# A four-layer transformer forward pass on one core: when a head's values run, when x rows are loaded, and how the decay and compressed-value products are shaped

## The chip, the core and the metric

The kernel runs on one core of a Trainium2 chip. A core has TensorE (matrix products, PE), VectorE (DVE), ScalarE (ACT), GpSimd (POOL) and SyncE (SP), each with a queue of its own that it works off in order, and DMA queues. The metric is device time in microseconds (us), lower is better. Before the change it is 2943.2 us, the median of three runs (2942.22 to 2947.26).

## The reference

One sequence of 512 tokens of 1024 values goes through two blocks of two layers each. The change touches the parts in bold.

```python
# first block: layer 0 mixes by dilated attention, layer 1 by a gated linear recurrence (LRU)
x = x + rms_norm(mixer(rms_norm(x, pre)), post)
x = x + rms_norm(conv_ffn(rms_norm(x, pre)), post)

# dilated attention: 3 groups of 8 heads of 128, each group with its own stride and band
logits = q k / sqrt(128) + bias, masked;  p = exp(logits - max);  o = p v / sum;  lse = max + log(sum)
alpha = softmax over the 3 groups of lse;  o = sum(alpha * o)          # then @ w_o

# conv_ffn: u = causal 3-tap convolution of x @ w_up; (gelu(g) * v) @ w_down

# second block, each layer: three mixers side by side
#   nsa:  8 heads, keys and values once compressed (blocks of 32), once selected, once in a window, gated
#   fox:  softmax(q k + c_i - c_j) v, c the running sum of log_sigmoid(f) of each head
#   memory: attention to 256 memory rows
```

In words: **the three groups of a head are merged by their maxima and sums**; **each layer ends with a norm, an addition to x and the next layer's norm**; **nsa adds the compressed values to the same accumulator as the other two**; **fox adds a decay c_i − c_j to each score**.

## The kernel before, in words

All large products run in three passes (`mm3`, L46 to L48): each operand is split into a high and a low part of the reduced fp32 format, and high by high, low by high and high by low are added in PSUM. A weight piece of 128 x 1024 is loaded by SP (`wunit`, L207), its high part cast by ScalarE (L197), its low part subtracted by VectorE (L198), or by POOL where the caller asks for it. `fms` (L218) makes products transposed, a column group at a time; the first call's group of several columns shares a pass over the tokens, and there the low parts of all columns but the first are made on POOL. `tm` (L238) makes the products that end a layer: four token blocks of 128, one PSUM bank each. `TOK_BANKS` (L38) names these: for the first half of the columns `acc`, `acc`, `acc`, `pv`. PSUM has three banks `acc`, two `sc`, two `tr` and one `pv`.

The program is written in the order of priority; a planner then lays out each engine's queue by its own simulated times. On the chip the engines keep that order and wait for each other by semaphores.

The attention (`dilated_attention`, L447) takes the query and key products of a head from `fms`, six of them (three groups, query and key), each 24 matmuls of 512 columns, 48 products in all. Scores of groups 1 and 2 (`DilatedHead.scores`, L79) are due one product after their group's key, those of group 0 one product after the head's last. A score adds the bias and takes the maximum on VectorE (L91, L100) and the exponential on ScalarE (L102). Groups order their rows differently, so the maxima and sums of each order (`own`) go to DRAM and come back in the other (L103, L104: `dx<-W` and `W<-dx`). `normalize` (L108) then works on the small tile `c`: VectorE L115 and L117, ScalarE L118 (exponential), VectorE to L122, and POOL scales `PA` and `PB`, the two orders' probabilities, by it (L126). `values` (L128) transposes these on TensorE (L136, L147), copies them out on ScalarE and VectorE, and multiplies them by the values into the bank `pv` (for the second order L155, L156), which VectorE adds to `oT` (L159). It is due `VALUES_AFTER` = 4 products after the head's last product. At the end all that is left is issued (`due(True)`, L494). `attn_layer` (L517) then splits `oT` and calls the output projection.

Each layer of the first block ends in `post_and_next` (L366): the product's first 512 columns for the four token blocks, then the second 512; from that, block by block, the sum of squares, the old x row (`x_load`, L352, two tiles in rotation, by SP), the new x (two operations at L390), its store, the next norm (L297 to L304), transposes (L312) and the split into the next layer's operands `hH`, `hL`.

In the second block the branches' work is woven with the products that build it. `fox` adds the decay to each score by a third matmul (L1268) of 4 rows: two rows hold the negated running sum's parts against ones, two the running sum's own. The four heads of a half lie at partitions 0, 32, 64 and 96, and the matmul names its place by `tile_position`. `decay` (L1277) fills the tile `A` of ones (POOL) and puts the rows in by eight DMAs per layer. `nsa` adds the compressed values by matmuls of 32 rows at `tile_position` (L1117), two per half of a head.

`colvec` (L267) loads up to 128 rows of a vector and transposes them (L277) to columns; `bias_tables` (L401) builds the relative bias with a table `oh` (L415).

Of the kernel before, what the change touches and what calls it, by code (L numbers as in the profile page):

```python
# [10 lines left out]
F32 = mybir.dt.float32  # L11
# [19 lines left out]
AHEAD = 0  # L31
VALUES_AFTER = 4
# [5 lines left out]
TOK_BANKS = (("acc", "acc", "acc", "pv"), ("sc", "sc", "tr", "tr"))  # L38
# [123 lines left out]
class Net:  # L162
    def __init__(self, ctx, tc, ins, out):
# [16 lines left out]
        self.junk = self.cp.tile([128, 512], mybir.dt.bfloat16, name="junk")  # L180
# [36 lines left out]
    def fms(self, w, cols, rh, rl, n=128, kt=KD, group=1, eng=None):  # L217
# [5 lines left out]
        q, ahead = 0, []  # L223
# [14 lines left out]
    def tm(self, w, col, n, lh, ll, kt=KD, banks=0, tail=0):  # L238
# [28 lines left out]
    def colvec(self, rows, name):  # L267

        nc = self.nc
# [6 lines left out]
        ps = self.bank("tr")  # L276
        nc.tensor.transpose(ps[:, :R], st, self.ident[:R, :R])  # L277
        out = self.vp.tile([128, R], F32, name=name)
        nc.vector.tensor_copy(out, ps[:, :R])
        return out  # L280
# [69 lines left out]
    def x_load(self, t):  # L350
        xt = self.ep.tile([128, D], F32, tag="nx", bufs=2, name="x")
        self.nc.sync.dma_start(xt, self.x[t * 128:(t + 1) * 128])  # L352
        return xt
# [12 lines left out]
    def post_and_next(self, w, lh, ll, kt, vectors, nxt, spare):  # L366
# [80 lines left out]
    def dilated_attention(self, qkv):  # L447
# [3 lines left out]
        oT = self.op.tile([128, KD, T], F32, tag="oT", bufs=1, name="oT")  # L451
# [18 lines left out]
        for hd in range(8):  # L470
# [22 lines left out]
            after(VALUES_AFTER, values, a)  # L493
        due(True)  # L494
        return oT

    def first_rows(self, g):

        with self.tc.tile_pool(name="edge", bufs=1) as self.ep:
            xs = [self.x_load(t) for t in range(2)]  # L500
# [3 lines left out]
            for t in range(NT):  # L504
                xt = xs[t] if t < 2 else self.x_load(t)
# [11 lines left out]
    def attn_layer(self, g_next, nxt):  # L517
        i, tc = self.i, self.tc
        with tc.tile_pool(name="attO", bufs=1) as self.op:
            self.ep = self.op  # L520
            with tc.tile_pool(name="attA", bufs=2) as self.ap:
                vs = self.post_vectors(i["norm_mix_post"][0], g_next)
                oT = self.dilated_attention(self.attn_qkv(self.h))
# [3 lines left out]
            with tc.tile_pool(name="attE", bufs=1) as self.ep:  # L527
                return self.post_and_next(i["attn_w_o"][0], *self.rows(oh), KD, vs, nxt,
                                          lambda i: self.ep.tile([128, T], F32, name=f"spare{i}"))
# [12 lines left out]
    def vectors(self):  # L542
# [4 lines left out]
        for l in range(2):  # L547
# [3 lines left out]
            for k, r in enumerate(rows):  # L551
                cols.append(self.colvec([r], f"cw{k}_{l}"))
# [3 lines left out]
        cv = self.colvec([i["lru_conv_w"][0].rearrange("k (r p) -> (k r) p", p=128), v8(i["lru_conv_b"][0]),  # L556
                          i["lru_ga_b"][0].rearrange("n (r p) -> (n r) p", p=128),
                          i["lru_gx_b"][0].rearrange("n (r p) -> (n r) p", p=128), v8(i["lru_lambda"][0])], "lrucv")
# [23 lines left out]
    def ffn_layer(self, l, up, g_next, nxt):  # L582
        nc, i, tc = self.nc, self.i, self.tc
        nf = FF // 128
        with tc.tile_pool(name=f"ffn{l}", bufs=1) as fp:
# [4 lines left out]
            for m in range(nf):  # L590
                u = []
                for c in (m, nf + m):
                    ps = next(up)
                    t = fp.tile([128, T], F32, tag="cv", bufs=6, name="cv")
                    self.conv(t, ps, lambda k: cw[k][:, c:c + 1], cb[:, c:c + 1], 3)
                    u.append(t)
                g, v = u
                nc.scalar.activation(g, g, AF.Gelu_apprx_tanh)
                nc.gpsimd.tensor_tensor(g, g, v, op=OP.mult)  # L599
                self.split(aH[m], aL[m], g)  # L600
            return self.post_and_next(i["ffn_w_down"][l], lambda k, t: aH[k][:, t * 128:(t + 1) * 128],
# [40 lines left out]
    def lru_layer(self, lin, g_next, nxt):  # L642
        nc, i, tc = self.nc, self.i, self.tc
        with tc.tile_pool(name="lru", bufs=1) as lp:
# [79 lines left out]
            ll = lambda k, t: xs[k // 2][1][:, k % 2, t * 128:(t + 1) * 128]  # L724
            return self.post_and_next(i["lru_w_out"][0], lh, ll, KD, self.post_vectors(i["norm_mix_post"][1], g_next), nxt, lambda i: lt("spare"))
# [84 lines left out]
    def zblocks(self, w, blocks, lh, ll, toks=NT):  # L810
# [8 lines left out]
        for t in range(toks):  # L819
            for (col, n, use), un in zip(blocks, us):  # L820
# [5 lines left out]
                zc = self.lt("zc", [128, n])  # L826
                nc.scalar.copy(zc, ps[:, :n])
                use(t, zc)
# [191 lines left out]
    def nsa(self, l, h, w_in, os):  # L1020
# [15 lines left out]
        def cmp_kv(t, z):  # L1036
# [16 lines left out]
        def key_value(br):  # L1053
            def use(t, z):
# [4 lines left out]
                if br == 1:  # L1059
                    nc.scalar.activation(gate[:, t], z[:, 256:280], AF.Tanh, scale=0.5)  # L1060
# [7 lines left out]
        def query(g):  # L1068
            def use(t, z):
# [23 lines left out]
        for p in range(4):  # L1093
            of = self.lt("of", [128, T])
            sl = self.silu2(l, h, OFF_NSILU + p * 128)
            for e in range(2):
                hd = 2 * p + e
                g, r = hd // 4, hd % 4
                for half in range(2):
# [15 lines left out]
                    rs = slice(32 * r, 32 * r + 32)  # L1115
                    for uu in range(2):
                        nc.tensor.matmul(ps[:, :256], VC[rs, g], PTC[rs, uu, g, hs], start=False, stop=False, tile_position=(32 * r, 0))  # L1117
# [5 lines left out]
    def compress(self, l, XT, gk):  # L1123
# [4 lines left out]
        VC = self.lt("VC", [128, 2, 128], F32R)  # L1128
        G = []
        for a, nm in ((0, "k"), (1, "v")):  # L1130
            pes = self.lt("pes", [16, 128])
# [322 lines left out]
```

## Time and profile before

| | before |
|---|---|
| median of three runs (lowest, highest) | 2943.2 us (2942.22, 2947.26) |
| the profiled execution: its time, its span | 2946.58 us, 2944.8 us |
| TensorE busy | 2816.7 us, 96% of the span |
| VectorE, ScalarE, POOL busy | 1647.3, 1303.5, 667.2 us |
| mean granted clock of TensorE | 0.979 |
| chain that ended last: PE, DVE, DMA, issue | 81%, 6%, 6%, 3% |

The profile is of one execution. "Busy" counts an engine's instructions, not its waiting. The chain that ended last is followed back from the last instruction, at each step to what released it. A wait is written as the waiting instruction, an arrow, and what ended the wait; "issue" is time in which nothing that the profile shows held the engine back. `PEclk` is the clock that TensorE was granted, 1.00 being full. Lines such as L136 are lines of the kernel. TensorE's matmuls overlap: the distance between starts tells what one costs, while its duration is longer.

### The profile page before, as it was taken

What the parts mean: (1) busy time and instruction counts of PE and PEld (TensorE: products, weight loads), DVE (VectorE), ACT (ScalarE), POOL (GpSimd) and SP (SyncE); (2) the same over time, 40 slices, a digit from 0 to 9 for tenths busy, and PEclk for the clock granted to TensorE, in tenths of its full rate; (3) what the DMA queues carried; (4) which work ended last, traced back from release to release, by engine and by line L of the source; (5) the groups of instructions that cost most, each with busy time, mean ns of one, the idle gap of its engine ahead of it and who ended that gap; (6) DMA issues with size and microseconds to landing.
All of it is one profiled execution on the core that took longest, in us unless ns stands there. A gap on an engine that the chain in (4) does not pass through costs nothing.

```text
span 2944.8 us, 40532 instructions
## 1 busy us (share of the span) xinstructions
PE 2816.7 (96%) x15005; PEld 2393.2 (81%) x15005; DVE 1647.3 (56%) x3232; ACT 1303.5 (44%) x2564; POOL 667.2 (23%) x754
## 2 busy tenths in 40 slices
PE   8998988799999997999999999999999999999999
PEld 7877777678888786888888898788888898788887
DVE  4235454465552459655524776666645667666653
ACT  4223343344442364444423654665533554665542
POOL 1001010121110225211101242334321352333320
PEclk9999999899999998999999999999999999999999
DMA  5453333153332342533323424112234423112233
GB/s 178 150 167 83 80 97 68 58 158 94 100 95 99 112 123 66 164 94 100 94 100 125 138 67 113 34 51 73 68 91 134 146 67 106 40 51 73 62 93 108
DMA packets 392317, 288.47 MB, mean 98 GB/s; under 512 B 33640, under 2 KB 351992, under 8 KB 392120
## 3 DMA queue, kind: packets, MB, share of 16 engines
q1 hardware_dynamic: 383120, 269.04, 31.7%
q10 hardware_dynamic: 9000, 16.85, 1.6%
q8 instruction: 119, 1.95, 0.3%
q14 instruction: 78, 0.64, 0.1%
HBM read 266.73 MB, written 21.07 MB: 98 GB/s over the span
## 4 chain that ended last, share of the span: by engine, by line
PE 81%; DVE 6%; DMA 6%; issue 3%; ACT 2%; POOL 2%; ACTq 0%; SPq 0%; DVEq 0%; POOLq 0%
PE acc L46 19%; PE acc L48 19%; PE acc L47 19%; PE tr L804 3%; DMA dx<-W 2%; PE pv L864 2%; PE sc L46 2%; PE sc L47 2%; PE sc L48 2%; PE tr L46 1%; PE tr L48 1%; PE tr L47 1%; PE pv L48 1%; PE pv L47 1%; PE pv L46 1%
## 5 line engine op out<-in xcount | busy, mean ns | idle before, releaser
L198 DVE TENSOR_TENSOR wl<-ws,wh 128x1024 fp32r<-128x1024 f32 (+4 forms) x456 | 543.3, 1192 | 620.0 <-ACT wh L197 615.8
L197 ACT CAST wh<-ws 128x1024 fp32r<-128x1024 f32 (+2 forms) x476 | 469.3, 986 | 724.9 <-PE acc L47 283.4
L46 PE MATMUL acc<-hH,wh 128*128 128x512 f32 (+1 forms) x1928 | 752.1, 391 | 23.1 <-ACT hH L197 13.6
L48 PE MATMUL acc<-hH,wl 128*128 128x512 f32 (+1 forms) x1928 | 748.1, 388 | 2.5 <-POOL wl L198 2.5
L47 PE MATMUL acc<-hL,wh 128*128 128x512 f32 (+1 forms) x1928 | 748.2, 388 | 1.0 <-DVE hL L198 0.9
L46 PEld LDWEIGHTS acc<-hH,wh 128*128 128x128 f32 x1928 | 368.5, 192 | 94.8 <-ACT hH L197 15.0
L48 PEld LDWEIGHTS acc<-hH,wl 128*128 128x128 f32 x1928 | 369.7, 192 | 74.3 <-POOL wl L198 4.1
L47 PEld LDWEIGHTS acc<-hL,wh 128*128 128x128 f32 x1928 | 369.1, 191 | 70.0 <-issue 2.3
L47 PE MATMUL acc<-wl,hH 128*128 128x256 f32 (+3 forms) x928 | 276.4, 299 | 0.7 <-DVE wl L198 0.6
L46 PE MATMUL acc<-wh,hH 128*128 128x256 f32 (+3 forms) x928 | 275.6, 299 | 0.3 <-ACT wh L197 0.3
L48 PE MATMUL acc<-wh,hL 128*128 128x256 f32 (+3 forms) x928 | 275.4, 299 | 0.0
L47 PEld LDWEIGHTS acc<-wl,hH 128*128 128x128 f32 x928 | 177.5, 192 | 6.5 <-DVE wl L198 1.2
L46 PEld LDWEIGHTS acc<-wh,hH 128*128 128x128 f32 x928 | 177.2, 192 | 6.7 <-ACT wh L197 0.7
L48 PEld LDWEIGHTS acc<-wh,hL 128*128 128x128 f32 x928 | 177.3, 192 | 4.3 <-DVE hL L198 0.2
L599 POOL TENSOR_TENSOR cv<-cv 128x512 f32<-128x512 f32 x48 | 62.0, 1292 | 464.1 <-DVE cv L540 448.6
L540 DVE SCALAR_TENSOR_TENSOR cv<-acc,cw,cv 128x511 f32<-128x511 f32 (+1 forms) x192 | 142.6, 746 | 3.2
L767 POOL TENSOR_TENSOR hst<-hst,mhalf 128x4 f32<-128x4 f32 (+2 forms) x90 | 92.8, 1035 | 203.7 <-DVE hst L766 197.7
L126 POOL TENSOR_SCALAR PA<-PA,c 128x256 f32<-128x256 f32 (+1 forms) x32 | 19.3, 621 | 511.4 <-DVE c L122 222.4
L837 ACT ACTIVATE P<-P,soft 128x128 f32<-128x128 f32 (+1 forms) x192 | 108.1, 564 | 61.0 <-DVE soft L836 58.7
L836 DVE CUSTOM_DVE_ANT_0 P<-sc,causal 128x128 f32<-128x128 f32 (+1 forms) x192 | 93.3, 487 | 69.2 <-PE tr L804 34.6
L804 PE MATMUL tr<-ident,P 128*128 128x128 f32 x720 | 125.0, 278 | 3.8 <-POOL P L1237 2.2
L839 POOL TENSOR_SCALAR P<-P,soft,ngate 128x128 f32<-128x128 f32 (+3 forms) x128 | 87.4, 688 | 146.7 <-DVE soft L838 120.0
(461 smaller groups left out, 5175.5 us busy)
## 6 DMA issues: line engine op xcount, KB each, us to landing
ws<-in_w_in_dram SPq DMA_DIRECT2D x116, 512.0 KB
ws<-in_ffn_w_up_dram SPq DMA_DIRECT2D x96, 512.0 KB
ws<-in_attn_w_qkv_dram SPq DMA_DIRECT2D x72, 512.0 KB
ws<-in_ffn_w_down_dram SPq DMA_DIRECT2D x48, 512.0 KB
x<-x ACTq DMA_DIRECT2D x16, 512.0 KB
ws<-in_lru_w_in_dram SPq DMA_DIRECT2D x16, 512.0 KB
ws<-in_w_mem_kv_dram SPq DMA_DIRECT2D x16, 512.0 KB
ws<-in_w_out_dram SPq DMA_DIRECT2D x16, 512.0 KB
```

The lines of the kernel that those rows point to most:

```text
L46: nc.tensor.matmul(out, lh, rh, start=start, stop=False)
L47: nc.tensor.matmul(out, lh, rl, start=False, stop=False)
L48: nc.tensor.matmul(out, ll, rh, start=False, stop=stop)
L197: nc.scalar.copy(hi, src)
L198: (eng or nc.vector).tensor_tensor(lo, src, hi.bitcast(F32), op=OP.subtract)
L540: nc.vector.scalar_tensor_tensor(dst[:, s:], ps[:, :T - s], cw(taps - 1 - s), dst[:, s:], op0=OP.mult, op1=OP.add)
L599: nc.gpsimd.tensor_tensor(g, g, v, op=OP.mult)
L767: nc.gpsimd.tensor_tensor(st[:, 1], st[:, 0], self.mhalf[:rows, :nh], op=OP.pow)
L804: self.nc.tensor.transpose(ps[:, a * 128:(a + 1) * 128], s, self.ident)
L836: nc.vector.tensor_tensor_reduce(out=P, in0=S, in1=self.causal[:, 512 - n:512], scale=-1.0, scalar=BIG, op0=OP.add, op1=OP.min, accum_out=m)
L837: nc.scalar.activation(P, P, AF.Exp, bias=m, scale=-1.0, accum_out=s)
L839: nc.gpsimd.tensor_scalar(P, P, r, mult, op0=OP.mult, op1=OP.mult)
```

## The change

It has these parts.

1. A head's values are due six products after its last one, not four. Head 7's are not issued at the end but returned as a closure. `tm` takes it as `hold`: it first issues the matmuls of all four token blocks for seven of the eight row pieces, then calls the closure (the values of head 7 and the split of the last piece of `oT`), then issues the last piece. For this call the four banks are `acc`, `acc`, `acc`, `sc`.
2. All four x rows are loaded after the first half's product is issued, before the second's, into tiles of the layer's other pools (`x_tile`); at the kernel's start all four are loaded before the norm's gain.
3. In `fms` the low parts of the first group's weights are made on VectorE. `AHEAD`, which was 0, is gone.
4. `colvec` splits into the load and the transpose, which comes one product later.
5. nsa's compressed values lie in a tile of 128 rows that is zero outside one head's 32, so that the matmul spans all 128 rows without `tile_position`.
6. fox writes the running sums to DRAM and, for each half of the heads, builds `AQ` (zeros, but for four rows a head) and `AK` (ones, but for two rows a head), 128 rows each; the matmul spans all 128 rows.
7. Temporaries change pools: the convolution's tiles in the ffn are pairs (four buffers), the recurrence's `xb` has four buffers, `zc` holds 256 columns and the gate columns are read from PSUM, and the compression's small tiles are taken from the rotating probability tiles.

```diff
-AHEAD = 0
-VALUES_AFTER = 4
+VALUES_AFTER = 6
-TOK_BANKS = (("acc", "acc", "acc", "pv"), ("sc", "sc", "tr", "tr"))
+TOK_BANKS = (("acc", "acc", "acc", "pv"), ("sc", "sc", "tr", "tr"), ("acc", "acc", "acc", "sc"))
...
-            us = ahead or [self.wunit(wv[:, :, c:c + n], self.nc.gpsimd if c != g[0] else eng) for c in g]
-            ahead = [self.wunit(wv[:, :, c:c + n], eng) for c in cols[q + len(g):q + len(g) + AHEAD]]
+            us = [self.wunit(wv[:, :, c:c + n], eng if q else None) for c in g]
...
-            for t in range(NT):
-                for k in range(k0, k0 + a):
-                    mm3(nc, ps[t][:, :n], lh(k, t), ll(k, t), wh[:, k - k0], wl[:, k - k0], k == 0, k == kt - 1)
+            ks = range(k0, k0 + a)
+            for ks in (ks[:-1], ks[-1:]) if hold and k0 + a == kt else (ks,):
+                if hold and ks[-1] == kt - 1:
+                    hold()
+                for t in range(NT):
+                    for k in ks:
+                        mm3(nc, ps[t][:, :n], lh(k, t), ll(k, t), wh[:, k - k0], wl[:, k - k0], k == 0, k == kt - 1)
...
-        y0 = [gained(t, 0, y) for t, y in enumerate(list(self.tm(w, 0, 512, lh, ll, kt=kt)))]
+        y0 = [gained(t, 0, y) for t, y in enumerate(list(self.tm(w, 0, 512, lh, ll, kt=kt, banks=2 if hold else 0, hold=hold)))]
+        xs = [self.x_load(t) for t in range(NT)]
         y1 = self.tm(w, 512, 512, lh, ll, kt=kt, banks=1, tail=4)
 
         def new_x(t, yg, y):
-            xt = self.x_load(t)
+            xt = xs[t]
...
-            after(VALUES_AFTER, values, a)
+            if hd < 7:
+                after(VALUES_AFTER, values, a)
         due(True)
-        return oT
+        return lambda: values(a)
...
-            xs = [self.x_load(t) for t in range(2)]
+            xs = [self.x_load(t) for t in range(NT)]
             gn = self.vec_bc(g)
...
-            for k in range(KD):
+            for k in range(KD - 1):
                 self.split(oh[0][:, k], oh[1][:, k], oT[:, k])
...
+            def hold():
+                last()
+                self.split(oh[0][:, KD - 1], oh[1][:, KD - 1], oT[:, KD - 1])
...
-                xb = lp.tile([128, 2, T], F32, tag="xb", bufs=3, name="xb")
+                xb = lp.tile([128, 2, T], F32, tag="xb", bufs=4, name="xb")
...
-                        nc.tensor.matmul(ps[:, :256], VC[rs, g], PTC[rs, uu, g, hs], start=False, stop=False, tile_position=(32 * r, 0))
+                        nc.tensor.matmul(ps[:, :256], VC[:, g, r], PTC[:, uu, g, hs], start=False, stop=False)
...
-                            nc.tensor.matmul(S[:, :n], A[rs, 0, hf, bs], A[rs, 1, hf, :n], start=False, stop=True, tile_position=(32 * hl, 0))
+                            nc.tensor.matmul(S[:, :n], AQ[:, hl, bs], AK[:, :n], start=False, stop=True)
...
-        nc.gpsimd.memset(A.bitcast(F32), 1.0)
-        Ab = A.bitcast(F32)
-        for hf in range(2):
-            for u in range(2):
-                nc.sync.dma_start(Ab[u::32, 1, hf], ck.bitcast(F32)[4 * hf:4 * hf + 4, u])
-                nc.sync.dma_start(Ab[2 + u::32, 0, hf], cq.bitcast(F32)[4 * hf:4 * hf + 4, u])
...
+    def decay_rows(self, hf):
+        nc = self.nc
+        AQ, AK = self.state([128, 4, T]), self.lt("fox_a", [128, T], F32R)
+        Q, K = AQ.bitcast(F32), AK.bitcast(F32)
+        nc.gpsimd.memset(Q, 0.0)
+        nc.gpsimd.memset(K, 1.0)
+        for u in range(2):
+            nc.sync.dma_start(K[u::32], self.cd[1, u, 4 * hf:4 * hf + 4])
+        for a in range(4):
+            nc.gpsimd.memset(Q[32 * a:32 * a + 2, a], 1.0)
+            nc.sync.dma_start(Q[32 * a + 2:32 * a + 4, a], self.cd[0, :, 4 * hf + a])
+        return AQ, AK
```

## Rows read from the trace of the kernel before

**Rows 1.** Waits of TensorE, whole span: us in total, times, longest us.

```profile
PE tr L136 <- POOL PA L126: 53.4, 8, 12.7
PE acc L46 <- ACT hH L197: 13.6, 6, 5.3
...
PE tr L277 <- DVE oh L415: 4.1, 1, 4.1
```

**Rows 2.** Stretches: start:end, length, busy us of each engine (instructions), PEclk, DMA.

```profile
146.00:540.00 394.00, 349.16 (x1695) 290.85 (x1694) 182.66 (x402) 141.39 (x278) 31.36 (x56) 0.93 0.38 98
223.50:230.50 7.00, 6.45 (x25) 5.54 (x25) 6.55 (x17) 2.27 (x4) 4.63 (x8) 0.55 0.40 118
516.00:527.60 11.60, 7.05 (x35) 6.25 (x36) 7.76 (x18) 4.85 (x9) 4.41 (x8) 0.71 0.26 92
534.30:552.40 18.10, 18.10 (x93) 15.07 (x92) 9.82 (x21) 7.26 (x17) 0.00 (x0) 1.00 0.16 31
552.40:587.40 35.00, 19.31 (x80) 15.94 (x80) 10.40 (x21) 7.62 (x14) 3.56 (x8) 0.71 0.17 57
615.00:622.40 7.40, 6.29 (x28) 6.03 (x29) 7.12 (x9) 4.93 (x10) 5.61 (x4) 0.54 0.47 158
1209.30:1216.30 7.00, 5.20 (x23) 4.94 (x24) 6.64 (x9) 5.73 (x12) 5.61 (x4) 0.51 0.40 140
2505.00:2945.00 440.00, 431.27 (x2433) 362.98 (x2431) 259.23 (x652) 213.29 (x502) 132.26 (x156) 1.00 0.25 70
```

**Rows 3.** Chain of waits from 355 to 380 us: start, us, what.

```profile
356.56 9.56 DMA dx<-W
...
366.13 2.72 DMA W<-dx
...
372.59 0.33 PE tr L136
```

**Rows 4.** Waits from 146 to 580 us: total, times, longest.

```profile
ACT c L118 <- DVE c L117: 83.6, 8, 13.7
DVE c L115 <- DMA W<-dx: 66.3, 6, 13.9
...
DVE c L115 <- issue: 27.7, 2, 13.9
```

**Rows 5.** TensorE's instructions at 2792 us: start, duration, line, operation.

```profile
2792.43 0.39 PE L1266 MATMUL sc<-st 128*128 128x512 f32 x1
2792.66 0.40 PE L1267 MATMUL sc<-st 128*128 128x512 f32 x1
2792.98 0.49 PE L1268 MATMUL sc<-st 4*128 4x512 f32 x1
2793.40 0.50 PE L46 MATMUL acc<-hH,wh 128*128 128x512 f32 x1
2793.74 0.39 PE L47 MATMUL acc<-hL,wh 128*128 128x512 f32 x1
```

**Rows 6.** VectorE's instructions at 606 to 612 us.

```profile
606.26 0.74 DVE L304 SCALAR_TENSOR_TENSOR spare<-x,st,gb 128x512 f32<-128x512 f32 x1
606.92 1.22 DVE L198 TENSOR_TENSOR wl<-ws,wh 128x1024 fp32r<-128x1024 f32 x1
608.05 4.52 DVE L390 SCALAR_TENSOR_TENSOR x<-spare,post_st,x 128x512 f32<-128x512 f32 x2
```

**Rows 7.** POOL's instructions, the same time.

```profile
609.23 2.80 POOL L198 TENSOR_TENSOR wl<-ws,wh 128x1024 fp32r<-128x1024 f32 x1
```

**Rows 8.** TensorE's instructions at 1857 us.

```profile
1856.50 0.54 PE L864 MATMUL pv<-pt,st 128*128 128x256 f32 x3
1856.97 0.50 PE L1117 MATMUL pv<-st,VC 32*128 32x256 f32 x2
...
1857.62 0.28 PE L1108 MATMUL sc<-st 128*128 128x256 f32 x1
```

**Rows 9.** Chain of waits at the start of the kernel.

```profile
1.64 6.15 DMA gb<-in_norm_mix_pre_dram
```

More of the change, by code (lines that the diff above doesn't have):

```diff
@@ L236, in fms, with tm @@
             q += len(g)
-    def tm(self, w, col, n, lh, ll, kt=KD, banks=0, tail=0):
+    def tm(self, w, col, n, lh, ll, kt=KD, banks=0, tail=0, hold=None):
         nc = self.nc
@@ L275, in colvec, with turn @@
             o += r.shape[0]
-        ps = self.bank("tr")
-        nc.tensor.transpose(ps[:, :R], st, self.ident[:R, :R])
         out = self.vp.tile([128, R], F32, name=name)
-        nc.vector.tensor_copy(out, ps[:, :R])
-        return out
+        def turn():
+            ps = self.bank("tr")
+            nc.tensor.transpose(ps[:, :R], st, self.ident[:R, :R])
+            nc.vector.tensor_copy(out, ps[:, :R])
+        return out, turn
     def rstd(self, ss, n, inv, k=1):
@@ L518, in attn_layer, with spare @@
         i, tc = self.i, self.tc
[L519 to L523, printed above, removed]
+        with tc.tile_pool(name="attO", bufs=1) as self.op, tc.tile_pool(name="attA", bufs=2) as self.ap:
+            ap, self.ep = self.ap, self.op
+            vs = self.post_vectors(i["norm_mix_post"][0], g_next)
+            self.ep = ap
+            oT = self.op.tile([128, KD, T], F32, tag="oT", bufs=1, name="oT")
+            last = self.dilated_attention(self.attn_qkv(self.h), oT)
             oh = self.new_h()
-            for k in range(KD):
+            for k in range(KD - 1):
                 self.split(oh[0][:, k], oh[1][:, k], oT[:, k])
-            with tc.tile_pool(name="attE", bufs=1) as self.ep:
-                return self.post_and_next(i["attn_w_o"][0], *self.rows(oh), KD, vs, nxt,
-                                          lambda i: self.ep.tile([128, T], F32, name=f"spare{i}"))
+            def hold():
+                last()
+                self.split(oh[0][:, KD - 1], oh[1][:, KD - 1], oT[:, KD - 1])
+            free = {}
+            def spare(i):
+                if i // 4 not in free:
+                    free[i // 4] = ap.tile([128, 4, T], F32R, tag="qk", bufs=4, name="spare").bitcast(F32)
+                return free[i // 4][:, i % 4]
+            tags = iter(("vH", "vL", "vH", "vL"))
+            self.x_tile = lambda: ap.tile([128, D], F32R, tag=next(tags), bufs=3, name="x").bitcast(F32)
+            return self.post_and_next(i["attn_w_o"][0], *self.rows(oh), KD, vs, nxt, spare, hold)
     @staticmethod
@@ L550, in vectors @@
             cols = []
-            for k, r in enumerate(rows):
-                cols.append(self.colvec([r], f"cw{k}_{l}"))
+            for k in (0, 2):
+                two = [self.colvec([r], f"cw{k + j}_{l}") for j, r in enumerate(rows[k:k + 2])]
+                yield
+                for out, turn in two:
+                    turn()
+                    cols.append(out)
                 yield
@@ L1034, in nsa, with cmp_kv @@
         QT = [None, None]
-        def cmp_kv(t, z):
+        def cmp_kv(t, z, more):
             cs = slice(t * 128, (t + 1) * 128)
@@ L1068, in query, with use @@
         def query(g):
-            def use(t, z):
+            def use(t, z, more):
                 qn = self.head_norm(z, 4, 64)
@@ L1181, in compress @@
                         nc.vector.tensor_copy(vf[32 * r:32 * r + 32, g], o[32 * g:32 * g + 32, :64])
-                self.split(VC[:, :, 0:64], VC[:, :, 64:128], vf)
+                for r in range(4):
+                    rs = slice(32 * r, 32 * r + 32)
+                    self.split(VC[rs, :, r, 0:64], VC[rs, :, r, 64:128], vf[rs])
                 yield VC
@@ L1218, in fox @@
         os.extend([None] * 4)
-        A = self.state([128, 2, 2, T])
+        self.cd = self.dp.tile([2, 2, 8, T], F32, name=f"cd{l}")
         f = self.lt("fox_f", [128, NT, 8])
@@ L1224, in fox, with value, key @@
             Q = self.state([128, 4, T])
-            def value(t, z):
+            def value(t, z, more):
                 self.split(V[:, t, :, 0:64], V[:, t, :, 64:128], z[:, :256].rearrange("p (h d) -> p h d", h=4))
                 if hf:
-                    nc.vector.tensor_tensor(f[:, t], z[:, 256:264], fb, op=OP.add)
+                    nc.vector.tensor_tensor(f[:, t], more, fb, op=OP.add)
                     if t == NT - 1:
-                        self.decay(f, A)
-            def key(t, z):
+                        self.decay(f)
+            def key(t, z, more):
                 kn = self.head_norm(z, 4, 64)
@@ L1332, in mkey, with use @@
         def mkey(c):
-            def use(t, z):
+            def use(t, z, more):
                 kn = self.head_norm(z, 2, 128)
```

85 lines of the change are left out of this document (45 added, 40 removed).

## The prediction

> **What bounds the kernel now.** I read the waits of TensorE first, then busy time by stretch, then the chain of waits inside the worst stretch, then single instructions. The kernel is bound by TensorE; the question is where it stands idle or runs slower than it could. The waits [rows 1] name few places: eight stalls on `PA` (53.4 us, the longest 12.7), six on `hH` at the ends of layers (13.6), one of 4.1 on `oh`. The stretches [rows 2] add the clock. In the attention, 146 to 540 us, TensorE is busy 349.16 of 394 us at a mean granted clock of 0.93, though 1.00 in undisturbed stretches; its levels are 1.2 and 2.4 GHz, so about 14% of the stretch ran at the lower one, right after the stalls. The last row of that view holds the second block's branches in its second layer: 431.27 of 440 us busy, clock 1.00. Little is idle there, so only cheaper TensorE work shortens it.
>
> The chain inside one head [rows 3] shows the stall's cause. The maxima go through DRAM: the write `dx<-W` takes 9.56 us and the read back 2.72. Then a few VectorE operations on `c`, a ScalarE exponential, POOL's scaling of `PA` and the first transpose at L136, which began at 372.59, 16.0 us after the write. VectorE and ScalarE stand in their queues for the same data [rows 4]: `c` at L115 waits 66.3 us in 6 cases and 27.7 in 2, 13.9 at most; `c` at L118 waits 83.6 in 8.
>
> **A, heads 0 to 6: 37 us.** A product is 24 matmuls of 512 columns at some 0.227 us between starts (the first interval of [rows 5] reads 0.23), 5.45 us. Values now come four products after a head; two more give 10.9 us, more than the longest of these seven waits (about 7; 53.4 − 12.7 = 40.7 in all), so the transposes no longer wait for POOL. What is late next is VectorE: while it waits for `c`, no product's result leaves PSUM. With three accumulator banks, TensorE covers two products, 10.9 us. A wait of 13.9 leaves 3.0 us, 21 over seven heads; the mean wait, (66.3 + 27.7) / 8 = 11.75, leaves 0.9, 6 in all. I take 14. The clock: in the first and last of the seven stall stretches [rows 2], 0.55 over 7.0 us means 6.3 us at the lower level, of which at most 0.55 idle, so (6.3 − 0.55) / 2 = 2.9 us of work time lost; 0.71 over 11.6 with 4.55 idle gives 1.1. Reading all seven in this way gives 13.7 as the least; I take back 10, since some stalls stay. 40.7 − 14 + 10 = 37. Bounds: 10 if the wait only moves (first rival), 50 if none stays.
>
> **B, the last head: 10 us.** The closure puts head 7's values behind seven eighths of the output projection's first half. But [rows 2] show that the projection already runs there: from 534.3 to 552.4 TensorE is busy for all 18.10 us, since three of four token blocks have their bank free (21 matmuls each). Only the fourth, whose bank `pv` is wanted by the values, waits; the 35 us after that hold 19.31 of work at clock 0.71. The new bank `sc` lets 21 × 0.227 = 4.8 us more run before the stall of 12.7. Head 6's values, two products later, put part of their work (about as much again) beside the softmax, but they also stand ahead of head 7's scores: I count 2.5. The clock: 20.3 of the 35 us at the lower level, 15.7 idle, so at least 2.3 lost. 4.8 + 2.5 + 2.3 = 9.6. Bounds 3 (nothing but part of the fourth block) and 16 (the whole stall and the clock).
>
> **C, layer boundaries: 11 us.** Three ends of layers carry most of the 13.6 us on `hH`; the clock adds at least (7.40 × 0.92 − 1.11) / 2 = 2.9 and (7.00 × 0.98 − 1.80) / 2 = 2.5 at the first and last of them [rows 2]. The change loads all x rows before the second half, and takes the first group's low halves of weights from POOL to VectorE. [Rows 6, 7] show why that matters: two updates of x that start at 608.05 need 4.52 us, beside POOL's 2.80 us for one low half; the weight operation on VectorE takes 1.22. The same operation on the same shape at L304, a little earlier, takes 0.74, so 3.0 us are lost; the like three times over is 9. Earlier rows and the clock give 2 more, plus what VectorE's extra 2 × 1.22 us takes away if it stands ahead of the update: three times 2.4 is 7, the lower bound 2. Above: all idle time and clock, 19.
>
> **D, matmuls of four and of 32 rows: 33 us.** In [rows 5] L1266 and L1267 start 0.23 us apart; the tiled L1268 starts 0.32 after L1267, the next matmul 0.42 after it, and the one behind 0.34 after that. Three intervals take 1.08 where three of 0.227 take 0.68: 0.40 too much, and the mean over 64 is 0.41, whatever the width. In [rows 8] a pair L1117 stands in a run of six 256-wide matmuls: from 1856.50 to L1108 at 1857.62 is 1.12 us where 6 × 0.12 would be 0.72: 0.40 for each of 32 pairs. 64 × 0.41 + 32 × 0.40 = 39 us, in stretches as busy as the last of [rows 2], 98%. The new full-row matmul should cost as the one before it, 0.23 at 512 columns. I take 33, since [rows 2] show 8.7 us idle already in 440, and faster TensorE meets more waits. Below: if only the tiled ones' own interval shrinks, 64 × 0.19 + 64 × 0.05 = 15. On TensorE's cost of switching, the Trainium skill's "TensorEngine Tiling (Array Packing)", Key Properties, says that a change of tiling mode drains the engine; this trace's 0.40 agrees. Its page "TensorE: Matmul & The Clock Gate", "Why this matters for your kernels", speaks against the change: a single matmul of 32 rows takes the time of a full one, the gain being in tiles that run together. By that alone D would be nothing; a rival below works it out.
>
> **E, the start: −3.5 us.** Two more rows of x (512 KB each by their shape) go ahead of the gain. It now lands 7.8 us in, behind two rows, 6.15 us after its issue [rows 9]: 1.5 MB by then, 0.19 MB/us. At that mean rate a megabyte more takes 5.2 us; the rate is higher once the queue runs, and rows that are there earlier may give it back: 0. It is a link of the chain that ended last, so it counts.
>
> **F, vector transposes: +1.** Their transposes come one product later; the 4.1 us on `oh` [rows 1] may go (bound 7 with its clock) or stay: its cause is another operation ahead on VectorE.
>
> **G, the rest: −2.** Per half of the forgetting heads POOL fills one 128 x 2048 state and smaller ones, where it filled one a layer, on an engine busy 132 of 440 us [rows 2]; SP issues 28 DMAs for 16. Two projections lie between these and their first reader. Tiles taken from other pools, one more `xb` buffer and the narrower `zc` remove and add waits that no row separates: −6 to 0, and I take −2.
>
> Sum: 37 + 10 + 11 + 33 − 3.5 + 1 − 2 = 86.5. The profiled execution took 2946.6 (span 2944.8); 2946.6 − 86.5 = 2860. It stands 3.4 above the median of 2943.2, on which the forecast is **2857 us**.
>
> **Rivals.**
> 1. The stall moves. The later values still need VectorE: their copies and the additions to `oT` queue behind `c` of the next head, so TensorE waits at `pv` for a wait of 12 us. For it: `c` blocks at every head [rows 4]. Against: the values precede the next head's scores by one product. A falls to 10: 2857 + 27 = 2884. Chance 0.20.
> 2. The tiled matmuls return nothing: their excess is the price of few rows being read, and a full matmul with another operand pays the same. For it: matmuls beside L1268 also have long intervals. Against: L1266 has 128 rows and 0.23. D = 0: 2890. Chance 0.06. It is what that rule of the Trainium skill would give.
> 3. Everything reaches its upper bound, with the stalls and their slower clock gone at once: 50 + 16 + 19 + 39 + 0 + 5 + 0 = 129 gives 2814; most of it, 2830. For it: no step needs another to fail. Chance 0.13.
> 4. Slower. If a head's values reach TensorE's queue just when `c` begins its wait, the products behind them can't run on free banks, and the whole wait is idle: 13.9 us × 7 = 97, with a third more for the clock (13.7 / 40.7) 130, in place of 40.7 + 13.7. A becomes −75 and the sum −25: 2968. It decides from some 11.1 us a head, where 7 × 11.1 × 1.33 eats 54 + 50 of the other terms. The mean wait of 11.75 would do; against it, the order puts that work a product earlier. Chance 0.03.
> That the last head's closure does not do what it says (B near 3, since the overlap is there) is inside the forecast's own range, 2843 to 2873.
>
> **Chances.** Forecast 0.56, rivals 0.20, 0.06, 0.13, 0.03; between no change and slower by small mishaps 0.02. A measurement of this kernel tells 0.2% (6 us) from no change. Faster 0.95, the same 0.02, slower 0.03. The range, 2824 to 2900, takes in the first two rivals and most of the third.
>
> **What would show it.** A: L136 waits for `PA` under 5 us in all, what is left stands at `acc` behind VectorE, and the clock of 146 to 540 us is 0.97 or more; rival 1 has waits at `pv`. B: 21 matmuls more before the stall, which is shorter than 6 us. C: updates of x of 0.75 us at the boundaries. D: L1266's intervals at what was L1268, and the two branch stretches some 16 us shorter each. E: the gain lands near 11 us. The prediction is wrong if the heads still show seven stalls of 5 us, or if the second block takes the same time.

## The result, and the profile after

The changed kernel takes 2912.41 us (median of four runs, 2909.61 to 2920.27) against 2943.96 before (median of four); the ratio is 0.9896 with a 95% interval of 0.9874 to 0.9917. A second measurement on another chip gave 0.9896 (0.9881 to 0.9911). It is faster, by 31.5 us and not the 86.5 of the forecast; 2857 and its range, 2824 to 2900, missed it.

Cut at the same landmarks, the two profiled executions (spans 2944.8 and 2907.7) show where:

| stretch | before | after | difference | forecast |
|---|---|---|---|---|
| start to the first query product | 146.1 | 149.8 | +3.7 | +3.5 (E) |
| 48 products of the heads | 388.6 | 374.1 | −14.5 | −38 (A, F) |
| last product to the first matmul of the feed-forward layer | 81.1 | 88.2 | +7.1 | −14 (B, a third of C) |
| rest of the first block | 1019.1 | 1015.6 | −3.5 | −7 (rest of C) |
| second block, both layers | 1309.9 | 1280.1 | −29.8 | −31 (D, G) |

The first three rows end at 615.8 us before and 612.1 after. Rows two and three don't hold the same work in both kernels: head 6's values, some 35 matmuls, have moved from the one to the other. Together they are 7.4 us shorter, where 52 were forecast. A single execution is not exact here, either. In experiments three and fifteen, whose TensorE order up to the second block is that of the changed kernel, the 48 products took 364.2 and 370.2 us, at a clock of 0.96 and 0.94, and the rest of the first block 1018.2 and 1017.7. So the second row's difference is −14 to −24 us, the fourth's −1 to −4. Waits of TensorE, whole span, changed kernel (total, times, longest):

```profile
PE sc L87 <- DVE qk L197: 14.6, 6, 4.0
PE acc L318 <- DVE xn L310: 12.0, 1, 12.0
PE acc L318 <- DVE spare L310: 10.4, 2, 9.8
PE acc L45 <- DVE c L119: 8.7, 3, 3.8
PE sc L46 <- DVE wl L197: 7.5, 2, 7.2
...
PE acc L45 <- ACT hH L196: 6.4, 6, 2.4
...
PE acc L45 <- DVE qk L200: 4.9, 3, 2.5
...
PE tr L284 <- DVE oh L422: 2.5, 1, 2.5
```

(Lines moved with the edit: mm3 is L45 to L47, the split L196 and L197, the score matmuls L87, `c` L114 to L121, POOL's scaling L125, the values' transposes L135.) The 53.4 us on POOL [rows 1] are gone; every large wait is now on VectorE. Stretches of the changed kernel, columns as in [rows 2]:

```profile
149.80:523.90 374.10, 341.12 (x1632) 282.10 (x1631) 172.47 (x383) 130.52 (x262) 46.28 (x56) 0.94 0.40 103
...
595.90:612.10 16.20, 4.10 (x21) 3.23 (x21) 14.63 (x27) 11.86 (x27) 8.75 (x10) 0.62 0.68 221
...
2478.00:2907.00 429.00, 420.39 (x2454) 364.45 (x2452) 264.50 (x669) 213.50 (x504) 142.19 (x169) 1.00 0.26 74
```

The heads' clock is 0.94 where it was 0.93: summed over pieces of 5 us, 48 us at the lower level are left of 55 (44 in experiment fifteen, 31 in three). The last row holds the second layer's branches to the end of the kernel, with 21 matmuls more than the last of [rows 2] in 11 us less, 98% busy as before.

At 313 us, VectorE's queue shows why the heads still stall. Chain of waits of the changed kernel (start, us, what):

```profile
299.65 11.80 DMA dx<-W
...
311.47 2.07 DMA W<-dx
...
313.56 0.18 DVE c L114
...
315.23 1.23 DVE wl L197
316.46 0.60 DVE qk L200
317.06 0.54 DVE oT L158
...
318.64 0.61 DVE oT L158
319.25 1.07 DVE vL L197
...
320.52 1.21 DVE wl L197
321.73 0.62 DVE qk L197
...
322.39 0.58 PE sc L87
```

The instruction at each end, VectorE's and TensorE's, with the idle time before it and what ended it in brackets:

```profile
313.56 0.17 DVE L114 TENSOR_TENSOR c<-W 128x8 f32<-128x8 f32 x1 [12.09 <-DMA W<-dx]
322.39 0.58 PE L87 MATMUL sc<-qk 128*128 128x256 f32 x1 [4.02 <-DVE qk L197]
```

VectorE waits for `c` from 301.5 to 313.56. Then it has 8.8 us of arrears (work that piled up behind the wait): weight halves, additions to `oT`, values. Only at 322.3 is the low half of `qk` ready that the next scores read. TensorE had work until 318.4, 16.9 us after VectorE began to wait. VectorE's waits from 192 to 518 us, changed kernel:

```profile
DVE c L114 <- DMA W<-dx: 50.1, 4, 13.6
...
DVE c L114 <- issue: 43.0, 3, 15.2
```

That is 93 us in seven heads, the amount of [rows 4] (94.0 in eight).

### The profile page after: what moved, and what is told of

The parts are those of the page before. It is cut to its first block, busy times and chain, and to the rows that moved or that the text cites. A ratio compares the mean times of both kernels' runs of the same rounds, so it can differ in the third digit from the quotient of the medians.

```text
span 2907.7 us, 40567 instructions
## 1 busy us (share of the span) xinstructions
PE 2784.3 (96%) x15005; PEld 2384.3 (82%) x15005; DVE 1646.0 (57%) x3245; ACT 1300.7 (45%) x2570; POOL 674.1 (23%) x771
## 4 chain that ended last, share of the span: by engine, by line
PE 78%; DVE 8%; DMA 6%; issue 3%; ACT 3%; POOL 1%; SPq 0%; ACTq 0%; DVEq 0%; POOLq 0%
PE acc L46 19%; PE acc L47 19%; PE acc L45 19%; PE tr L832 3%; PE pv L892 2%; PE sc L46 2%; PE sc L45 2%; PE sc L47 2%; DMA dx<-W 2%; DVE wl L197 2%; PE tr L45 1%; PE tr L47 1%; PE tr L46 1%; PE pv L47 1%; PE pv L46 1%
## 5 line engine op out<-in xcount | busy, mean ns | idle before, releaser
L197 DVE TENSOR_TENSOR wl<-ws,wh 128x1024 fp32r<-128x1024 f32 (+5 forms) x463 | 553.8, 1197 | 627.6 <-ACT wh L196 624.6
L196 ACT CAST wh<-ws 128x1024 fp32r<-128x1024 f32 (+2 forms) x476 | 469.3, 986 | 719.1 <-PE acc L46 275.1
L45 PE MATMUL acc<-hH,wh 128*128 128x512 f32 (+1 forms) x1928 | 750.1, 390 | 28.0 <-DVE c L119 8.7
L47 PE MATMUL acc<-hH,wl 128*128 128x512 f32 (+1 forms) x1928 | 746.7, 388 | 2.5 <-POOL wl L197 2.5
L45 PEld LDWEIGHTS acc<-hH,wh 128*128 128x128 f32 x1928 | 368.0, 191 | 99.9 <-issue 22.8
L47 PEld LDWEIGHTS acc<-hH,wl 128*128 128x128 f32 x1928 | 368.5, 191 | 73.4 <-POOL wl L197 3.8
L45 PE MATMUL acc<-wh,hH 128*128 128x256 f32 (+3 forms) x928 | 277.1, 300 | 2.0 <-ACT hH L196 2.0
L47 PE MATMUL acc<-wh,hL 128*128 128x256 f32 (+3 forms) x928 | 276.4, 300 | 0.1
L45 PEld LDWEIGHTS acc<-wh,hH 128*128 128x128 f32 x928 | 178.6, 193 | 7.2 <-ACT hH L196 2.2
L47 PEld LDWEIGHTS acc<-wh,hL 128*128 128x128 f32 x928 | 178.3, 192 | 4.6 <-DVE hL L197 0.6
L125 POOL TENSOR_SCALAR PA<-PA,c 128x256 f32<-128x256 f32 (+1 forms) x32 | 23.9, 763 | 492.0 <-ACT qk L196 205.1
```

The costliest lines, as they stand in the source:

```text
L45: nc.tensor.matmul(out, lh, rh, start=start, stop=False)
L47: nc.tensor.matmul(out, ll, rh, start=False, stop=stop)
L196: nc.scalar.copy(hi, src)
L197: (eng or nc.vector).tensor_tensor(lo, src, hi.bitcast(F32), op=OP.subtract)
```

## The experiments

Ratios are to the kernel before on the same chip; the changed kernel's is 0.9896.

**One: values at four products again.**

```diff
-VALUES_AFTER = 6
+VALUES_AFTER = 4
```

> The changed kernel, but a head's values again four products after the head (head 7's still held). Theory (VectorE and ScalarE waiting in their queues for c pace the heads, whichever place the values have): the wait of L135 on POOL comes back with some 35 to 40 us, the waits at acc and sc that replaced it (29 us) mostly go, and the time is 8 to 16 us above the changed kernel's 2912, so 2920 to 2928. Rival (the later values are worth their 37 us and something else in the change took it back): 2940 to 2950.

Measured: 2925.45 us, ratio 0.9946 (0.9932 to 0.9959), 0.51% or 15 us slower than the changed kernel. L135 waits for POOL 38.8 us in seven heads again. So moving the values is worth 15 us in this program: removing a wait of 40 us uncovered another of 30.

**Two: c behind the fourth product.** A one-column copy ties `c` to that product's result; in the trace TensorE's order is the changed kernel's, matmul for matmul, up to the second block.

```diff
-        if order == 0:
-            self.normalize()
...
+        if ps is not None:
+            nc.vector.tensor_copy(c[:, 0, 0, 1, 0:1], ps[:, 0:1])
         nc.vector.tensor_tensor(r, nm[:, :, 0], nm[:, :, 1], op=OP.min)
...
             after(1, a.scores, qk, 0)
+            after(4, norm, a)          # norm calls a.normalize(bank of the current product)
```

> The changed kernel, but the work on c (normalize) is tied to the fourth product after the head, by a one-column copy from that product's bank into c, so that VectorE's queue holds the copies and weight halves of the products in between ahead of c; TensorE's order stays as it is. Theory (VectorE blocked by c is what idles TensorE in heads 0 to 6): waits of TensorE between 192 and 518 us fall from 29 us to under 10, the low-clock stretches from six to at most two, the wait of VectorE on W<-dx from 93 us to under 15; 25 to 40 us faster than the changed kernel, 2872 to 2887. Rival (the products are short of weights or of SyncE, which waits for the same write to DRAM): the stalls move to waits on weight pieces and the time stays at 2905 to 2915.

Measured: 2867.61 us, 0.9762 (0.9748 to 0.9776): 1.35% or 39 us faster than the changed kernel. TensorE's waits from 192 to 481 us, then the stretch of all heads, then VectorE's wait:

```profile
PE sc L87 <- DVE qk L197: 1.1, 3, 0.6
PE sc L87 <- DVE W L99: 1.1, 1, 1.1
```

```profile
149.80:480.90 331.10, 324.79 (x1632) 271.05 (x1632) 173.90 (x390) 131.40 (x262) 30.48 (x56) 0.99 0.45 116
```

```profile
DVE c L114 <- DMA W<-dx: 27.6, 7, 4.7
```

The 30.3 us of waits in the heads (14.6 + 8.7 + 4.9 and 2.1 for the maxima of L99) are 2.2, the clock is 0.99, and the 48 products take 331.1 us, 43 less than in the changed kernel's profile (33 and 39 less than in those of experiments three and fifteen). The same 1632 matmuls are 16 us less busy, which is the clock given back. VectorE's wait on the read back did not fall under 15 us, as expected, but to 27.6; the gain is there all the same. The rival, that SyncE or the weights were short, falls: SyncE still waits for the same write, 80.5 us in the heads where it was 80.9.

**Three: the tiled matmuls.**

```diff
-  nc.tensor.matmul(S[:, :n], AQ[:, hl, bs], AK[:, :n], start=False, stop=True)
+  nc.tensor.matmul(S[:, :n], AQ[32*hl:32*hl+4, hl, bs], AK[32*hl:32*hl+4, :n], start=False, stop=True, tile_position=(32*hl, 0))
...                                     (and the same, over 32 rows, for VC and PTC)
```

> The changed kernel with its zero-padded tiles, but each decay matmul reads only its 4 rows and each matmul of compressed values only its 32, at their tile position, as before. Theory (the form of the matmul is worth what the second block gained): the two layers of the second block become 16 and 14 us longer, 2938 to 2944 in all. Rival (a single matmul of few rows takes the time of a full one, as the Trainium skill's page TensorE: Matmul & The Clock Gate has it, and the gain came from the other order of the work): within 6 us of the changed kernel's 2912.

Measured: 2936.79 us, 0.9994 (0.9985 to 1.0004), 0.99% or 29 us slower. Its second block's two layers:

```profile
1619.60:2284.50 664.90, 653.96 (x4015) 568.67 (x4015) 434.84 (x1047) 345.65 (x803) 224.37 (x289) 1.00 0.30 86
2284.50:2929.00 644.50, 632.89 (x3835) 547.73 (x3835) 412.47 (x1008) 324.02 (x756) 218.56 (x275) 1.00 0.28 80
```

1309.4 us in all, where the changed kernel has 1280.1 and the kernel before 1309.9, with the zero padding, POOL's fills and the DMAs of the changed kernel in place. The form of the matmul is the gain. In the changed kernel, in place of the intervals of [rows 5]:

```profile
2748.47 0.39 PE L1297 MATMUL sc<-st 128*128 128x512 f32 x1
2748.70 0.40 PE L1298 MATMUL sc<-fox_a,st 128*128 128x512 f32 x1
2748.94 0.39 PE L46 MATMUL acc<-hL,wh 128*128 128x512 f32 x1
2749.17 0.40 PE L47 MATMUL acc<-hH,wl 128*128 128x512 f32 x1
```

Three intervals of 0.23 or 0.24, where they were 0.32, 0.42 and 0.34.

**Four: the waiting block last.** In the output projection's second half, two of four blocks use `sc`, and one `sc` is still held by the first half's fourth block, which the change put there.

```diff
+  TOK_BANKS[3] = ("sc", "tr", "tr", "sc")
-  y1 = self.tm(w, 512, 512, lh, ll, kt=kt, banks=1, tail=4)
+  y1 = self.tm(w, 512, 512, lh, ll, kt=kt, banks=3 if hold else 1, tail=4)
```

> The changed kernel, but the second half of the attention's output projection uses the banks sc, tr, tr, sc for its four token blocks, not sc, sc, tr, tr, so that the block that must wait for the bank of the first half's fourth block is the last one, not the second. Theory (the second block's late end at 596 us bunches the norm work of three blocks behind it, which makes the 9.8 us stall at 608): the stretch from the last matmul of the projection to the first of the feed-forward layer shrinks from 16 us to about 8, and the time by 6 to 10, to 2902 to 2906. Rival (the stall is the length of ScalarE's and VectorE's work for the norms, wherever the banks are): 2909 to 2915.

Measured: 2901.81 us, 0.9876 (0.9863 to 0.9890), 6 us below the changed kernel's ratio, at the edge of what two such intervals tell apart. The traces are clearer. TensorE's stalls at the layer's end, changed kernel, then this one (the bracket is the idle time and what ended it):

```profile
608.01 1.11 PE L318 MATMUL acc<-ident,spare 128*128 128x128 f32 x4 [9.77 <-DVE spare L310]
610.43 1.97 PE L318 MATMUL sc<-ident,spare 128*128 128x128 f32 x8 [1.31 <-POOL spare L308]
```

```profile
594.79 1.97 PE L318 MATMUL acc<-ident,spare 128*128 128x128 f32 x8 [6.84 <-DVE spare L310]
...
605.56 0.50 PE L45 MATMUL acc<-hH,wh 128*128 128x256 f32 x2 [0.99 <-ACT hH L196]
```

The projection's last matmul starts at 595.5 us in the changed kernel, 16.6 us ahead of the next layer's first; here at 603.75, 1.8 us ahead. The bank order was the cause of the long end, but a stall of 6.84 in the middle stays.

**Five to eight: the smaller parts, one at a time.** No hold (head 7's values ahead of the projection, bank `pv`); x rows loaded where they are used; the first group's low halves on POOL; two x rows at the start.

```diff
five: attn_layer, post_and_next
+            hold()
             free = {}
...
-  self.tm(w, 0, 512, lh, ll, kt=kt, banks=2 if hold else 0, hold=hold)
+  self.tm(w, 0, 512, lh, ll, kt=kt, banks=0)
six: post_and_next
-        xs = [self.x_load(t) for t in range(NT)]
...
-            xt = xs[t]
+            xt = self.x_load(t)
seven: fms
-  self.wunit(wv[:, :, c:c + n], eng if q else None)
+  self.wunit(wv[:, :, c:c + n], self.nc.gpsimd if c != g[0] else eng)
eight: first_rows
-            xs = [self.x_load(t) for t in range(NT)]
+            xs = [self.x_load(t) for t in range(2)]
...
-                xt = xs[t]
+                xt = xs[t] if t < 2 else self.x_load(t)
```

> The changed kernel, but head 7's values and the last split come ahead of the output projection again, whose fourth block is back in bank pv. Theory (the hold shortens the stall on head 7 but pays for it at the next layer's start, where the second block of the projection's second half waits for the bank sc): the stall on POOL is about 12 us again, the one at 608 us about 5, and the time within 4 us of the changed kernel's (0.9896 of before). Rival (the hold is worth the 10 us that were forecast): 7 to 12 us slower, 0.992 to 0.994 of before.

> The changed kernel, but each x row is loaded where its block is worked off, as before (into the changed kernel's tiles). Theory (the rows' early load hides nothing that was on the path, since before no engine waited for a row at the boundaries): within 3 us of the changed kernel. Rival (it is a good part of the 11 us of term C): 4 to 9 us slower.

> The changed kernel, but the low halves of the first group's weights are made on POOL again. Theory (the contention is real, but the time it took is small against the chain of norms): the updates of x beside POOL's weight halves take up to 2.8 us again, and the time is 1 to 5 us above the changed kernel. Rival (term C as forecast, of which this was 9 us): 7 to 10 us slower. Second rival (VectorE's extra 2.4 us at each boundary took it all back): no change.

> The changed kernel, but at its start two x rows are loaded ahead of the gain, the other two as their tiles come, as before (four tiles). Theory (the gain's landing sets the first matmul): the first matmul comes 3.2 us earlier, near 8.7, and the time is 2 to 4 us below the changed kernel. Rival (the later rows give it back before 146 us): no change.

Measured: 0.9887 (0.9870 to 0.9903), 0.9899 (0.9883 to 0.9914), 0.9911 (0.9895 to 0.9926) and 0.9887 (0.9868 to 0.9905). The point values are 3 us faster, 1 slower, 4 slower and 3 faster; none can be told from 0.9896 by time. The first still excludes the forecast's 10 us for the hold. Without the hold, TensorE's one stall on head 7:

```profile
552.85 0.47 PE L135 MATMUL tr<-ident,PA 128*128 128x128 f32 x1 [10.67 <-POOL PA L125]
```

and 2.99 us at the layer's end. With it, 7.23 and 9.77: what the hold saves in one place it loses in the other. For the low halves, two updates of x at the next boundary (VectorE's instructions; changed kernel, then with POOL):

```profile
1007.91 1.41 DVE L397 SCALAR_TENSOR_TENSOR x<-spare,post_st,x 128x512 f32<-128x512 f32 x2 [0.44 <-POOL post_st L348]
```

```profile
1005.31 5.64 DVE L397 SCALAR_TENSOR_TENSOR x<-spare,post_st,x 128x512 f32<-128x512 f32 x2 [1.17 <-POOL post_st L348]
```

POOL's weight halves in the same moment, with POOL:

```profile
1005.25 5.16 POOL L197 TENSOR_TENSOR wl<-ws,wh 128x1024 fp32r<-128x1024 f32 x2
```

The updates take 4.2 us more beside them. The rest of the first block takes 1021.6 us in this profile, where it took 1015.6 and 1017.7 in the changed kernel's two; the point value of the time is 4 us up. With two rows first, the first matmul comes at 8.83 us, not 11.95.

**Nine to eleven: together.** c behind the product, with two rows first and the bank order (nine); with two rows first and no hold (ten); as nine, with head 7's `c` tied to the fourth weight piece of the projection (eleven).

```diff
nine: the edits of two, four and eight; ten: those of two, five and eight; eleven: nine's, and
-                    hold()
+                    hold(wh[:, 0].bitcast(F32))     # a.normalize(that), then the values
```

> The changed kernel with three edits together: c behind the fourth product (1.35% faster than the changed kernel alone), the banks sc, tr, tr, sc (0.2%), two rows of x first (0.1%). Theory (the three have places of their own, at the heads, at the end of the projection, at the start): the gains add, 39 + 6 + 3 = 48 us below the changed kernel, a ratio to before of 0.971 to 0.975. Rival (a stall that goes in one place is found again in the next, as with the values): 0.976 or more.

> The same without the hold: head 7's values ahead of the projection, bank pv for the fourth block and the old banks for the second half. Theory (hold and new bank together are worth the 6 us of the bank order): 3 to 9 us slower than with hold and bank order. Rival (without the hold the layer's end is as good): within 3 us.

> The first of these three, and head 7's c tied to the fourth weight piece of the output projection (a one-column copy from its high half), so that VectorE makes the weight halves ahead of it. Theory (the 6.5 us stall in the projection is VectorE blocked by c, too): the wait on wl there goes, and the time is 4 to 9 us below the one without. Rival (the values then come late, and the wait moves to L135 on POOL): no change, or up to 5 us slower.

Measured: 2871.98 us, 0.9742 (0.9729 to 0.9756); 2869.56, 0.9732 (0.9719 to 0.9745); 2870.76, 0.9738 (0.9724 to 0.9751). All three beat both kernels, the changed one by 1.5% and more. Nine is where it was expected, but its gain over experiment two (0.9762) is too small to be sure of, and the three can't be told from each other. That ten is as fast as nine was not expected: the hold is not needed. Eleven's edit did not bind: VectorE's instructions show the copy at 493.56 us, before the scores ended, and `c` again ahead of the weight halves:

```profile
516.74 0.17 DVE L114 TENSOR_TENSOR c<-W 128x8 f32<-128x8 f32 x1 [10.43 <-DMA W<-dx]
516.94 0.24 DVE L116 TENSOR_TENSOR c<-c,W 128x8 f32<-128x8 f32 x2
517.10 1.22 DVE L197 TENSOR_TENSOR wl<-ws,wh 128x1024 fp32r<-128x1024 f32 x1
```

So what head 7's stall is worth stays open.

**Twelve to fifteen: the two edits of the heads alone, in the kernel before.** Values at six products (twelve); `c` tied to the fourth product (thirteen); both (fourteen); the changed kernel beside the last two (fifteen).

```diff
twelve (thirteen: the edit of experiment two, in the kernel before; fourteen: both)
-VALUES_AFTER = 4
+VALUES_AFTER = 6
```

> The kernel before with one number changed, the values of a head six products after it instead of four; nothing else of the change. Theory (term A is 11 to 15 us, not 37, since VectorE's wait for c stands behind the values' wait): 9 to 17 us faster than before, 0.994 to 0.997. Rival (A is 37, and other parts of the change cost 20): 30 to 40 us faster, 0.987 to 0.990.

> The kernel before, values four products after the head as they were, with only c tied to the fourth product. Theory (two waits stand one behind the other, VectorE's for c and the values' for POOL, and either alone holds a head back): c now comes just ahead of the values, L136 still waits for POOL's scaling of PA, 4 to 7 us a head; the time is within 12 us of before, 0.996 to 1.003. Rival (the place of c is worth its 40 us by itself): 0.983 to 0.988.

> The kernel before with both: c tied to the fourth product, values six products after the head; nothing else of the change. Theory (both waits gone, so the heads run through): waits of TensorE in heads 1 to 6 under 8 us, low-clock time there near none, 42 to 55 us faster than before, 0.981 to 0.986. Rival (in this program the head's end takes it back, as with the values alone): 0.990 or more.

> The changed kernel as it is, once more, beside the two above on the same chip: 0.9874 to 0.9917 of before if the first measurement stands.

| | values at 4 | values at 6 |
|---|---|---|
| `c` as it was | 1 | 0.9998 (0.9989 to 1.0007) |
| `c` behind the fourth product | 0.9871 (0.9855 to 0.9888) | 0.9837 (0.9823 to 0.9852) |

Fifteen gave 0.9896 again. Both of my expectations on the single edits fell. The values alone gain nothing in this program, not 9 to 17 us. The edit on `c` alone gains 38 us, not 12 at most: the rival was right there. In thirteen, L136 waits for POOL 13.4 us in all, 9.4 of it head 7. That edit moved more than `c`: the planner also put the values' transposes 13 to 16 product matmuls later, some 3 us a head, which hides part of POOL's wait. But twelve moved them later still and gained nothing, and in experiment two, with TensorE's order unchanged, the place of `c` gained 39 us. Both together gain 48 us, as expected (42 to 55): once VectorE is not blocked, the later values add 10. The two waits do not stand as equals behind each other: VectorE blocked by `c` is most of the loss. Twelve shows the exchange, with TensorE's waits from 146 to 529 us:

```profile
PE sc L88 <- DVE qk L198: 17.7, 6, 5.1
PE acc L46 <- DVE c L120: 9.8, 3, 4.0
PE acc L46 <- DVE qk L201: 7.6, 3, 3.2
```

35 us, for the 40.7 that went [rows 1]. Its 48 products took 383.1 us (388.6 before), and the stretch behind them 86.4 (81.1), where head 6's values now are.

## Why the prediction was wrong, step by step

**A, 37 us: wrong, and most of the miss.** The step that failed is the overlap, "TensorE covers two products, 10.9 us", set against VectorE's wait alone, and with it "I take 14": 30.3 us were idle, 24 and 28 in the profiles of experiments fifteen and three. The transposes did stop waiting for POOL, and what was late next was VectorE waiting for `c`, as named; its size was wrong, on three counts.
- The stall does not end with `c`. VectorE then works off 8.8 us of arrears before the operand that TensorE wants, and I counted only the wait. At 313 us TensorE's cover was even longer than I took, 16.9 us, and the wait of 12.1 alone would have been hidden; wait and arrears, 20.9, left 4.0 idle.
- The banks do not bound it alone. The scores of the next head stand in TensorE's queue and read `qk`, whose low half is among the arrears; they wait 14.6 us, more than the 13.6 at the banks.
- With these stalls, in pieces of up to 4 us, the clock came back only in part: 7 us less at the lower level, worth some 3, where I counted 10 (5 in fifteen, 12 in three).

Measured, A was 15 us in the changed kernel (undone) and nothing in the kernel before (done alone). Where these two differ shows in the traces: with the values at six the heads have 35 us of such waits and 62 us at the lower level in twelve, 24 to 30 and 31 to 48 in the three profiles with the changed kernel's heads. Why they do stays open. What term A needed is shown: with `c` moved as well, the two edits gave 48 us, near its upper bound of 50. The first rival had the mechanism, a wait moved behind VectorE's `c`, but put it at `pv`. I weighed it at 0.20 on the ground that the values come a product earlier, which says nothing about the scores.

**B, 10 us: wrong.** The shorter stall came (12.7 to 7.2, under 6 forecast), with the wait at a weight half, VectorE again. But the 4.8 us that the new bank `sc` lets run left out who wanted that bank next: the second half's second block waited for it and came last, so the norms of three blocks bunched up behind it, and the time from the projection's last matmul to the next layer's first grew from 6.6 to 16.6 us. Experiments four and five show both sides. The +7.1 of the table is not all the bank's: head 6's values now stand in that stretch, which alone made it 5.3 longer in experiment twelve. But without the hold, with the same values in it, experiment five's is 82.5 us, where fifteen's with the hold is 87.4: by the traces the hold cost more than it saved, and by time it was worth nothing that can be told.

**C, 11 us: wrong, about 4 by the point value of experiment seven, which time alone can't tell from nothing.** The contention was real: the updates take 0.7 us each and 2.8 beside POOL. The Trainium skill's "SBUF — State Buffer", "SBUF: two separate sides", has a lock that VectorE and POOL share and that one holds for a whole instruction; the 5.64 against 1.41 us agrees. I took the loss three times over at full size; by experiment seven it was on the path about once. Loading the x rows early was worth nothing that could be measured, for at the boundaries no engine had waited for them.

**D, 33 us: right**, 29 by the runs, 29.3 by the two layers' lengths. On the single matmul of few rows, the rule of the Trainium skill's "TensorE: Matmul & The Clock Gate", "Why this matters for your kernels", that it takes a full one's time, did not hold here among full matmuls: each one or pair cost 0.4 us more by [rows 5, 8]. The "drain" of the Trainium skill's "TensorEngine Tiling (Array Packing)", Key Properties, agrees. Of the 39 us that these 0.4 make in all, 29 came back.

**E, +3.5: right** (+3.7 at the first product). With two rows first it comes at 147.2 us, 2.6 earlier, and the time is 3 us less by experiment eight's point value. F was small, as forecast: the wait on `oh` is 2.5, of 4.1. G is in no run by itself. In the third rival's sum F stands with 5, where its bound was 7; nothing hangs on it.

## What to carry to other kernels

When a wait is to go, ask what the engine behind it has queued: a blocked in-order engine costs its wait and its arrears, and all who read from the arrears. Here the wait seen on TensorE was the end of a chain, and the edit that paid 38 us moved a few small VectorE operations behind a later product's work, tied by data, since the planner's own times had put them up to 15 us ahead of the data that comes back from DRAM. When a tile gets another bank, list who takes that bank next, and in which order.

## What the runs showed of the hardware that was not expected

POOL's scaling of `PA` and `PB` took 46.3 us in 56 operations in the changed kernel's heads (46.3 in twelve's, too) and 31.4 in those of the kernel before (30.5 with `c` behind the product). It is slow where it falls beside VectorE's arrears: the eight at 315 us took 8.6 us, where eight take 4.5 at the mean of the kernel before. That the two contend, as in experiment seven, is likely, but was not tried here.
